# A hybrid decoder step on one core: the last 288 tokens of the end turned with tokens on partitions, h fetched back tile by tile, and the key row rooms given back later

## The chip, the cores and the metric

The program runs on one core of a Trainium2 chip. The metric is the time of one execution of the whole program in microseconds (us). TensorE (PE), VectorE (DVE), ScalarE (ACT) and GpSimd (POOL) each run their own stream of instructions in order; SyncE (SP) issues nearly all the transfers.

## The reference

One layer of a decoder for 512 prompt tokens, 32 sample tokens (8 sequences of 4) and 16 meta tokens, 560 in all, with a model width of 1024:

```python
h = x + 0.5 * rms_norm(swiglu(rms_norm(x, ffn1_pre_g), ...ffn1...), ffn1_post_g)
u = rms_norm(h, mix_pre_g); proj = u @ w_in
# a gated linear attention branch and a stick-breaking attention branch over proj
m = sigmoid(gate_a) * (o_a @ w_o_gla) + sigmoid(gate_b) * (o_b @ w_o_sb)
h = h + rms_norm(m @ w_out, mix_post_g)
y = h + 0.5 * rms_norm(swiglu(rms_norm(h, ffn2_pre_g), ...ffn2...), ffn2_post_g)
```

with `rms_norm(x, g) = x * rsqrt(mean(x*x) + eps) * g` over the width. Outputs are y of the prompt and of the samples (the meta tokens have none), the new keys and values, and the states of the linear attention. Only the last line, the fetch of h ahead of the two `h + ...` sums of the feed-forward blocks, and the writing of the new keys are touched here.

## The kernel before

Activations lie transposed: the width is cut into eight tiles of 128 partitions (`k` = 0 to 7, `hT[k]`), and the tokens are the columns (`NT` = 560 in the first block; `NW` = 544 from the mixer on, as the meta tokens end there). Every product in full precision is three TensorE matmuls of float32r operands split in a high and a low part (lines 681 to 697 and 1145 to 1147), so TensorE runs through the whole program.

The work on PE, DVE, ACT and POOL is in an order written out by hand (`tc.manual_schedule`): a matmul loop calls `step()` after each k-tile, and `later(n, f)` lets `f` emit its instructions n steps on; `flush()` steps until the list is empty. SP is not in that list: the order of the transfers in its queue is set by the framework's scheduler, and the queue itself is in order, so a transfer whose room or buffer isn't free yet holds those behind it.

On-chip room comes from an `Arena` of 150 units of 280 columns in chunks of six. `take(width)` hands out the free units that were given back longest ago, preferring single holes for single units; `give` returns them. A new user of a room waits for the last readers of it.

**Fetching h back.** While the feed-forward block runs, h lies in DRAM (`h_dram`). Both down projections (`Down.pair` for output tiles 2 and 3, and 4 and 5 in the second block; then `k_steps` loops of 22 steps for each remaining output tile and half of the tokens) call `h_again` two steps after the last pair: it takes three rooms and issues the eight loads of `hT[k]` (128x560, 280 KB each) at once, line 1191. The weights of the down projection come through three `raw` buffers (line 185); ACT copies a buffer to a high part (line 660) and DVE makes the low part (line 152).

**The end.** The tokens are in two halves of 272 columns. For each output tile n and half h, `Norm.tile` squares the product (ACT, line 739), scales it by the gain (ACT, line 740) into y, and DVE adds up the squares. When the last tile of a half is there, `start` sums the squares over the partitions with two matmuls against ones (lines 756 and 757; the sum comes out repeated on all partitions), ACT takes Ln and Exp(-0.5 ...) (lines 759 and 760), and for each of three sets of k-tiles (3, 3 and 2) `add` multiplies y by 1/rms and adds it to h on DVE (line 152). `out(j, g)` then turns 128 tokens j of set g on PE (line 2531), copies the turned rows out of PSUM (line 2532, ACT but for one) and writes them (line 2534). In the first half all this lies under the matmuls of tiles 7 and 6 of the second half. For the second half it comes after the last matmul: `start(1)`, and three times an `add` and the turns of token blocks 2, 3 and the 32 samples.

**Key rows.** In the attention part each pair of heads turns the keys of the 48 sample and meta tokens to rows `tk` (`tails`, lines 1885 to 1890), writes them with two DMAs and gives the room back right behind the issue.

Of the kernel before, what the change touches and what calls it, by code (L numbers as in the profile page):

```python
# [12 lines left out]
AF = mybir.ActivationFunctionType  # L13
ALU = mybir.AluOpType

P = 128
D = 1024
KD = D // P
NP = 512
NS = 32  # L20
NM = 16
NT = NP + NS + NM
HW = NT // 2
# [21 lines left out]
MIXER += [("S", "a", 4), ("R", "p", 2), ("R", "p", 3), ("S", "b", 4), ("S", "a", 6), ("R", "p", 4), ("R", "p", 5), ("S", "b", 6)]  # L45
MIXER += [("R", "p", 6), ("R", "p", 7)]
AHEAD = 150
SPREAD = 15
UNITS = 150


class Arena:
# [6 lines left out]
    def __init__(self, pool, n):  # L59
        self.pool, self.clock, self.made = pool, 0, 0  # L60
        self.freed = [[0] * self.CHUNK for _ in range(n // self.CHUNK)]
        self.tile = [None] * len(self.freed)
        self.held = {}
        self.keep = 0

    def take(self, width, dt=F32, tight=False):
        k = -(-width // self.UNIT)
        best = None
        empties = sum(None not in f for f in self.freed)
        for c, free in enumerate(self.freed):  # L70
            empty = None not in free
            if not empty and self.tile[c].dtype != dt:
                continue
            for s in range(self.CHUNK - k + 1):
                f = free[s : s + k]
                if None in f:
                    continue
                since = max(f) if not empty else max(free) + SPREAD
                waste = k % 2 == 0 and s % 2
                alone = k == 1 and free[s ^ 1] is not None  # L80
                key = (empty and empties <= self.keep, waste, tight and sum(x is not None for x in free), alone, since)
                if best is None or key < best[0]:
                    best = (key, c, s)
        assert best is not None, f"no room for {width}: {[sum(x is not None for x in f) for f in self.freed]}"
        _, c, s = best
        if None not in self.freed[c] and (self.tile[c] is None or self.tile[c].dtype != dt):
            self.made += 1
            self.tile[c] = self.pool.tile([P, self.CHUNK * self.UNIT], dt, tag=f"room{c}", name=f"room{c}_{self.made}")
        self.freed[c][s : s + k] = [None] * k
        a = self.tile[c][:, s * self.UNIT : s * self.UNIT + width]  # L90
        self.held[id(a)] = (a, c, s, k)
        return a
# [9 lines left out]
    def give(self, *aps):  # L102
        for a in aps:
            _, c, s, k = self.held.pop(id(a))
            self.clock += 1
            self.freed[c][s : s + k] = [self.clock] * k
# [14 lines left out]
def hybrid_step(  # L121
# [8 lines left out]
    nc = tc.nc  # L130
# [5 lines left out]
    V, S, G, T = nc.vector, nc.scalar, nc.gpsimd, nc.tensor  # L136
    arena = Arena(cp, UNITS)
    take, give = arena.take, arena.give
# [21 lines left out]
    hT, hT_room = whole(KD)  # L160
# [168 lines left out]
    class Head:  # L329
# [246 lines left out]
        def out(self, e):  # L576
            hd, p = self.hd, self.po
            if e < 2:
                oa[hd, e] = take(NP + NS)
                S.activation(oa[hd, e][:, :NP], p, AF.Copy, scale=g_gla[:, e : e + 1])  # L580
            else:
                for e in range(2):
                    S.activation(oa[hd, e][:, NP:], p[:, NS * e : NS * e + NS], AF.Copy, scale=g_gla[:, e : e + 1])
                give(*self.on)
# [132 lines left out]
    def later(n, f):  # L717
        todo.append([n, f])

    def flush():  # L720
        while todo:
            step()

    class Norm:
# [37 lines left out]
        def add(self, h, g):  # L762
# [5 lines left out]
            if g == 2:  # L768
                give(self.rs[h])

    class Gain:


# [410 lines left out]
        for i in range(len(waiting) + 3):  # L1184
            later(2 * i + 1, lambda: waiting and hidden(*waiting.pop(0), 1, nw, wid, hid, pairs))

    def h_again():
        nonlocal hT_room
        hT[:], hT_room = whole(KD)
        for k in range(KD):  # L1190
            nc.sync.dma_start(hT[k], h_dram[k])

    class Down:

# [160 lines left out]
    with tc.manual_schedule(engines={E.PE, E.DVE, E.Activation, E.Pool}):  # L1355
# [167 lines left out]
        for n, hs, j in by_chunks(order1):  # L1523
            if hs is None:
                down1.pair(n, ("ps", "acc"), True)
                later(2, h_again)
                continue
            if j == 0:
                accs[n, hs] = {h: ps("acc") for h in hs}
            acc, (k0, k1) = accs[n, hs], CUTS[j]  # L1530
            if j == 0 and n in EARLY and hs != (1,):
                st.fetch_early(*vrows[EARLY[n]])
            if (n, hs) == (7, (1,)):
                parts = last[j]
            else:
                parts = last[j] = st.parts.pop(0)

            ahead_ = {(7, (0,)): (1, 0, 0), (7, (1,)): (0, 1, 1), }.get((n, hs), (1, 1, 1))
            for _ in range(ahead_[j]):
                st.split()  # L1540
                st.fetch()
            k_steps(acc, parts, k0, k1, KF, hid, hs)
            if j < 2:
                continue
            for h in hs:
                later(1, lambda n=n, h=h, acc=acc: n1.tile(n, h, acc[h]))
            if (n, hs) == (7, (0,)):
                later(2, exp_ln_table)
            for h in range(2):
                if (n, hs) == ((7, (0,)), (4, (1,)))[h]:  # L1550
                    for k in range(KF):
                        give(*hid.t[k, h])
                    todo.extend([d, f] for d, f in g1.pieces(n1, h, *(F0, F1)[h]))
# [189 lines left out]
    class Pair:  # L1743
# [133 lines left out]
        def tails(self):  # L1877
            pr, kf, vf = self.pr, self.kf, self.vf
            p = ps()
            T.transpose(p[:NTL, :P], kf[:, :NTL], ident)  # L1880
            T.transpose(p[:NTL, P : 2 * P], vf[:, NP:], ident)
            T.transpose(p[:, 2 * P : 3 * P], vfm[pr % 2], ident)
            fc = slice(P * (pr % 4), P * (pr % 4) + P)
            self.vm = vm = take(P)
            tk = take(P)
            V.tensor_copy(tk[:NTL], p[:NTL, :P])
            c = slice(self.c0, self.c0 + P)
            nc.sync.dma_start(k_sample.rearrange("o b t h d -> (o b t) (h d)")[:, c], tk[:NS])
            nc.sync.dma_start(kp_out[:NM, c], tk[NS:NTL])
            give(tk)  # L1890
            V.tensor_copy(tail_v[pr // 4][:NTL, fc], p[:NTL, P : 2 * P])
            V.tensor_copy(vm, p[:, 2 * P : 3 * P])
            give(kf, vf)
# [402 lines left out]
    with tc.manual_schedule(engines={E.PE, E.DVE, E.Activation, E.Pool}):  # L2296
# [220 lines left out]
        early_tiles(u2, rs2, W2, NW, hid, pairs, {(0, 0): 9, (1, 0): 9}, lambda: next(feed2))  # L2517
        list(feed2)

        nd, last, accs = Norm(half2, (NW // 2, NW // 2)), {}, {}  # L2520
        down2 = Down(hid, NW, nd)
        down2.pieces(*DSUMS2)
        ys = y_sample.rearrange("b t d -> (b t) d")

        def out(j, g):

            n, ks = P if j < 4 else NS, Norm.SETS[g]
            w = P * len(ks)
            p, t = ps(), take(3 * P)
            for i, k in enumerate(ks):  # L2530
                T.transpose(p[:n, P * i : P * i + P], hT[k][:, P * j : P * j + n], ident)
            (V.tensor_copy if g == 2 and j == 3 else S.copy)(t[:n, :w], p[:n, :w])
            c = slice(P * ks[0], P * ks[0] + w)
            nc.sync.dma_start(y_prompt[0, P * j : P * j + n, c] if j < 4 else ys[:, c], t[:n, :w])

        for n, hs, j in by_chunks(order2):
            if hs is None:
                down2.pair(n, ("ps", "acc") if n == 2 else ("acc", "ps"), n == 4)
                if n == 4:
                    later(2, h_again)  # L2540
                continue
            if j == 0:
                accs[n, hs] = {h: ps("ps" if (n, hs) == (6, (0,)) else "acc") for h in hs}
            acc, (k0, k1) = accs[n, hs], CUTS[j]
            if (n, hs) == (7, (1,)):
                parts = last[j]
            else:
                parts = last[j] = st.parts.pop(0)
            for _ in range({(7, (0,)): (1, 0, 0), (7, (1,)): (0, 1, 1)}.get((n, hs), (1, 1, 1))[j]):
                ahead()  # L2550
            k_steps(acc, parts, k0, k1, KF, hid, hs, wid=nd.wid)
            if j < 2:
                continue
            for h in hs:
                later(1, lambda n=n, h=h, acc=acc: nd.tile(n, h, acc[h]))
            if (n, hs) == (7, (0,)):
                later(2, exp_ln_table)
                later(F1[0], lambda: nd.start(0))
                for g in range(3):
                    later(F1[1] + 9 * g, lambda g=g: nd.add(0, g))  # L2560
                    for j in range(2):
                        later(F1[1] + 9 * g + 7 + 4 * j, lambda j=j, g=g: out(j, g))
        for p in pairs.values():
            give(*p)
        later(2, lambda: nd.start(1))
        for g in range(3):
            later(3 + g, lambda g=g: (nd.add(1, g), [out(j, g) for j in (2, 3, 4)]))
        flush()


# [30 lines left out]
```

## Time and profile before

| | |
|---|---|
| Time, median of 3 runs | 1509.87 us (1509.79 to 1510.43) |
| The profiled execution | 1510.1 us |
| Its span, first to last instruction | 1508.4 us |
| Granted TensorE clock, mean | 0.999 |
| Busy: PE, DVE, ACT, POOL | 1494.6, 1090.8, 773.3, 149.0 us |
| Last matmul of the down projection ends | 1495.1 us after the start of the span |

The profiled execution takes 1.7 us more than its span, and 0.2 us more than the median of the runs. Times inside a trace are counted from the start of its span. A row of the chain or the timeline has the start, the length, the engine, the line and what was written from what; in brackets stands the idle time before it and what ended that. A row of a group has its count, its busy time in us and the mean of one in ns. In the windows the last three numbers are the clock granted to TensorE, the share of the DMA engines and GB/s.

### The profile page before, as it was taken

What the parts mean: (1) busy time and instruction counts of PE and PEld (TensorE: products, weight loads), DVE (VectorE), ACT (ScalarE), POOL (GpSimd) and SP (SyncE); (2) the same over time, 40 slices, a digit from 0 to 9 for tenths busy, and PEclk for the clock granted to TensorE, in tenths of its full rate; (3) what the DMA queues carried; (4) which work ended last, traced back from release to release, by engine and by line L of the source; (5) the groups of instructions that cost most, each with busy time, mean ns of one, the idle gap of its engine ahead of it and who ended that gap; (6) DMA issues with size and microseconds to landing.
All of it is one profiled execution on the core that took longest, in us unless ns stands there. A gap on an engine that the chain in (4) does not pass through costs nothing.

```text
span 1508.4 us, 29660 instructions
## 1 busy us (share of the span) xinstructions
PE 1494.6 (99%) x11923; PEld 1440.9 (96%) x11923; DVE 1090.8 (72%) x1934; ACT 773.3 (51%) x1425; POOL 149.0 (10%) x216
## 2 busy tenths in 40 slices
PE   9999999999999999999999999999999999999997
PEld 8999999999999889899888899999999999999997
DVE  5888888853787867877776434977567898888544
ACT  6455454533665557565555343634565555455333
POOL 2000000000000011123324541000000000000000
PEclk9999999999999999999999999999999999999999
DMA  8133333336565473334555568335531333332352
GB/s 250 53 88 99 98 98 97 88 103 193 155 158 149 121 110 85 91 85 115 128 107 141 177 202 196 92 99 144 156 107 67 99 98 99 99 110 87 94 163 85
DMA packets 276794, 180.40 MB, mean 120 GB/s; under 512 B 10202, under 2 KB 261648, under 8 KB 276656
## 3 DMA queue, kind: packets, MB, share of 16 engines
q1 hardware_dynamic: 271200, 161.64, 40.6%
q0 software_dynamic: 5440, 16.85, 3.3%
q8 instruction: 94, 1.54, 0.4%
q14 instruction: 44, 0.36, 0.1%
q10 hardware_dynamic: 16, 0.00, 0.0%
HBM read 155.72 MB, written 22.74 MB: 118 GB/s over the span
## 4 chain that ended last, share of the span: by engine, by line
PE 95%; DVE 2%; DMA 1%; ACT 1%; issue 0%; ACTq 0%; DVEq 0%; SPq 0%
PE acc L681 8%; PE acc L1147 8%; PE acc L1145 8%; PE acc L682 8%; PE acc L684 8%; PE acc L1146 8%; PE acc L694 7%; PE acc L697 7%; PE acc L695 7%; PE acc L1088 2%; PE acc L1085 2%; PE acc L1086 2%; PE acc L925 1%; PE acc L927 1%; PE acc L926 1%; PE ps L1920 1%
## 5 line engine op out<-in xcount | busy, mean ns | idle before, releaser
L152 DVE TENSOR_TENSOR lo<-raw,hi 128x1024 fp32r<-128x1024 f32 (+1 forms) x213 | 254.9, 1197 | 127.5 <-ACT hi L660 104.1
L152 DVE TENSOR_TENSOR room<-room,room 128x544 fp32r<-128x544 f32 (+17 forms) x419 | 266.2, 658 | 89.1 <-ACT room L760 27.9
L681 PE MATMUL acc<-room,hi 128*128 128x280 f32 (+1 forms) x928 | 271.2, 309 | 0.2 <-DVE room L155 0.2
L1147 PE MATMUL acc<-room,lo 128*128 128x280 f32 (+1 forms) x896 | 259.8, 290 | 0.0
L1146 PE MATMUL acc<-room,hi 128*128 128x280 f32 (+1 forms) x896 | 259.2, 289 | 0.0
L1145 PE MATMUL acc<-room,hi 128*128 128x280 f32 (+1 forms) x896 | 259.1, 289 | 0.0
L682 PE MATMUL acc<-room,hi 128*128 128x280 f32 (+1 forms) x928 | 250.4, 289 | 0.0
L684 PE MATMUL acc<-room,lo 128*128 128x280 f32 (+1 forms) x928 | 192.7, 289 | 0.0
L681 PEld LDWEIGHTS acc<-room,hi 128*128 128x128 f32 x928 | 174.8, 188 | 13.1 <-issue 11.0
L682 PEld LDWEIGHTS acc<-room,hi 128*128 128x128 f32 x928 | 175.1, 189 | 2.8 <-issue 1.9
L1147 PEld LDWEIGHTS acc<-room,lo 128*128 128x128 f32 x896 | 168.6, 188 | 0.0
L1145 PEld LDWEIGHTS acc<-room,hi 128*128 128x128 f32 x896 | 168.5, 188 | 0.0
L1146 PEld LDWEIGHTS acc<-room,hi 128*128 128x128 f32 x896 | 168.5, 188 | 0.0
L856 ACT CAST hi<-raw 128x1024 fp32r<-128x1024 f32 x92 | 96.4, 1052 | 133.1 <-PE acc L1146 48.7
L660 ACT CAST hi<-raw 128x1024 fp32r<-128x1024 f32 (+1 forms) x121 | 122.6, 1014 | 71.2 <-DMA raw<-in_ffn_w_down_dram 21.0
L684 PEld LDWEIGHTS acc<-room,lo 128*128 128x128 f32 x928 | 145.0, 188 | 0.0
L694 PE MATMUL acc<-room,hi 128*128 128x280 f32 (+2 forms) x498 | 143.0, 294 | 0.3 <-ACT hi L660 0.3
L695 PE MATMUL acc<-room,hi 128*128 128x280 f32 (+2 forms) x498 | 140.9, 290 | 0.0
L697 PE MATMUL acc<-room,lo 128*128 128x280 f32 (+2 forms) x498 | 127.8, 291 | 1.3 <-DVE lo L152 1.3
L856 ACT CAST hi<-room 128x1024 fp32r<-128x1024 f32 x84 | 70.2, 836 | 81.0 <-PE acc L1146 59.1
L694 PE MATMUL acc<-room,room 128*128 128x280 f32 (+3 forms) x366 | 107.8, 295 | 0.0
L152 DVE TENSOR_TENSOR lo<-room,hi 128x1024 fp32r<-128x1024 f32 x84 | 80.2, 955 | 37.0 <-ACT hi L856 36.8
(381 smaller groups left out, 3290.7 us busy)
## 6 DMA issues: line engine op xcount, KB each, us to landing
raw<-in_w_in_dram SPq DMA_DIRECT2D x49, 512.0 KB
raw<-in_ffn_w_down_dram SPq DMA_DIRECT2D x40, 448.0 KB
raw<-in_ffn_w_gate_dram SPq DMA_DIRECT2D x64, 256.0 KB
raw<-in_ffn_w_up_dram SPq DMA_DIRECT2D x64, 256.0 KB
out_dram<-room SPq DMA_DIRECT2D x32, 256.0 KB
raw<-in_ffn_w_down_dram SPq DMA_DIRECT2D x14, 512.0 KB
raw<-in_w_in_dram SPq DMA_DIRECT2D x28, 256.0 KB
h_dram<-room SPq DMA_DIRECT2D x24, 280.0 KB
```

Of the source, the lines that this page charges most:

```text
L152: (eng or V).tensor_tensor(out=out, in0=a, in1=b, op=op)
L660: S.copy(h_, src)
L681: T.matmul(acc[h][:, : wid[h]], hi[k], a[h][0], start=(k == 0), stop=False)
L682: T.matmul(acc[h][:, : wid[h]], hi[k], a[h][1], start=False, stop=False)
L684: T.matmul(acc[h][:, : wid[h]], lo[k], a[h][0], start=False, stop=(k == KD - 1))
L694: T.matmul(acc[h][:nw, : wid[h]], wh, a[h][0], start=(k == 0), stop=False)
L695: T.matmul(acc[h][:nw, : wid[h]], wh, a[h][1], start=False, stop=False)
L697: T.matmul(acc[h][:nw, : wid[h]], wl, a[h][0], start=False, stop=(k == kt - 1))
L856: S.copy(hi[:, :kt], src)
L1145: T.matmul(x[:, :QW], hi, act[k][0], start=(first and k == 0), stop=False, skip_group_check=True)
L1146: T.matmul(x[:, :QW], hi, act[k][1], start=False, stop=False, skip_group_check=True)
L1147: T.matmul(x[:, :QW], lo, act[k][0], start=False, stop=(k == 3), skip_group_check=True)
```

## The change

- `Last` takes the place of `Norm` in the second feed-forward block. Its y and sums of squares cover all 544 columns in shared rooms. The first part (`start`, `add` with columns 0 to 255, `out` for token blocks 0 and 1) is done where it was, for 256 columns instead of 272.
- The last 288 columns are done in `end`, behind the last matmul: the token blocks A (256 to 383) and B (384 to 511) and the samples C (512 to 543). h is turned by itself into SBUF (`x_turned`), y is turned by itself and stays in PSUM (`turned(y_at, ...)`). The squares of a token are summed by a matmul with the squares as the stationary operand and one column of ones, which gives one value per token on that token's partition, and one DVE instruction per 512 columns makes `y * rs + x` from PSUM and SBUF, written out as 128 rows of 512. Only the samples are multiplied and added as before (32 columns), turned, copied and written in two pieces.
- The last square goes with a DVE instead of an ACT scaling of y.
- `h_again(every)` spreads the eight loads: one each 8 steps in the first block, one each 5 steps in the second.
- `tk` is given back 12 steps later.

```diff
@@ -45,6 +45,7 @@
 MIXER += [("S", "a", 4), ("R", "p", 2), ("R", "p", 3), ("S", "b", 4), ("S", "a", 6), ("R", "p", 4), ("R", "p", 5), ("S", "b", 6)]
 MIXER += [("R", "p", 6), ("R", "p", 7)]
 AHEAD = 150
+LEAVE = 12
 SPREAD = 15
 UNITS = 150
 
@@ -768,6 +769,108 @@
             if g == 2:
                 give(self.rs[h])
 
+    class Last:
+
+        A = 2 * P
+
+        def __init__(self, post, w):
+            self.wid, self.w, self.post, self.n, self.y, self.q = (w, w), w, post, [0, 0], {}, {}
+
+        def view(self, g):
+            return self.y[g].rearrange("p (k t) -> p k t", t=NT)
+
+        def tile(self, n, h, acc):
+            w, g = self.w, n // 3
+            c = slice(h * w, h * w + w)
+            if g not in self.y:
+                self.y[g] = take(len(Norm.SETS[g]) * NT)
+            self.n[h] += 1
+            what = {1: "sum", KD: "last"}.get(self.n[h])
+            if what:
+                if what not in self.q:
+                    self.q[what] = take(NT)
+                q = self.q[what][:, c]
+            else:
+                q_ = take(HW)
+                q = q_[:, :w]
+            S.activation(q, acc[:, :w], AF.Square)
+            y = self.view(g)[:, n % 3, c]
+            if h and self.n[h] == KD:
+                V.tensor_scalar(out=y, in0=acc[:, :w], scalar1=self.post[:, n : n + 1], scalar2=None, op0=ALU.mult)
+            else:
+                S.activation(y, acc[:, :w], AF.Copy, scale=self.post[:, n : n + 1])
+            if not what:
+                tt(self.q["sum"][:, c], self.q["sum"][:, c], q, ALU.add)
+                give(q_)
+
+        def start(self):
+            w = self.A
+            rs = self.rs = take(w)
+            p = ps()
+            T.matmul(p[:, :w], ones, self.q["sum"][:, :w], start=True, stop=False)
+            T.matmul(p[:, :w], ones, self.q["last"][:, :w], start=False, stop=True)
+            S.activation(rs, p[:, :w], AF.Ln, bias=epst, scale=1.0 / D)
+            S.activation(rs, rs, AF.Exp, scale=-0.5)
+
+        def add(self, g, c, rs):
+            n = len(Norm.SETS[g])
+            y, x = self.view(g)[:, :, c], hT_room[g].rearrange("p (k t) -> p k t", t=NT)[:, :n, c]
+            tt(y, y, rs.unsqueeze(1).to_broadcast([P, n, c.stop - c.start]), ALU.mult)
+            tt(x, x, y, ALU.add)
+
+        def end(self, prompt, samples):
+            def turned(src, c, n, w):
+                p = ps("acc")
+                for i in range(4):
+                    T.transpose(p[:n, P * i : P * i + P], src(4 * w + i)[:, c : c + n], ident)
+                return p
+
+            def x_at(k):
+                return hT[k]
+
+            def y_at(k):
+                return self.view(k // 3)[:, k % 3]
+
+            def x_turned(c):
+                t = take(D)
+                for w in range(2):
+                    p = ps()
+                    for i in range(4):
+                        T.transpose(p[:, P * i : P * i + P], hT[4 * w + i][:, c : c + P], ident)
+                    S.copy(t[:, 512 * w : 512 * w + 512], p)
+                return t
+
+            def out(c, w, y, x, r):
+                o = take(512)
+                stt(o, y, r, x[:, 512 * w : 512 * w + 512], ALU.mult, ALU.add)
+                nc.sync.dma_start(prompt[c : c + P, 512 * w : 512 * w + 512], o)
+
+            A, B, C = self.A, self.A + P, NP
+            q, rs = self.q["sum"], take(P)
+            xa = x_turned(A)
+            tt(q[:, A:NW], q[:, A:NW], self.q["last"][:, A:NW], ALU.add)
+            ya = [turned(y_at, A, P, 0)]
+            p = ps()
+            for i, c in enumerate((A, B)):
+                T.matmul(p[:, i : i + 1], q[:, c : c + P], ones[:, :1], start=True, stop=True)
+            T.matmul(p[:, 2 : 2 + NS], ones, q[:, C:NW], start=True, stop=True)
+            S.activation(rs[:, : 2 + NS], p[:, : 2 + NS], AF.Ln, bias=epst, scale=1.0 / D)
+            S.activation(rs[:, : 2 + NS], rs[:, : 2 + NS], AF.Exp, scale=-0.5)
+            ya.append(turned(y_at, A, P, 1))
+            out(A, 0, ya[0], xa, rs[:, 0:1])
+            xb = x_turned(B)
+            out(A, 1, ya[1], xa, rs[:, 0:1])
+            for g in range(3):
+                self.add(g, slice(C, NW), rs[:, 2 : 2 + NS])
+            yb = [turned(y_at, B, P, w) for w in range(2)]
+            pc = [turned(x_at, C, NS, w) for w in range(2)]
+            out(B, 0, yb[0], xb, rs[:, 1:2])
+            for w in range(2):
+                t = take(512)
+                S.copy(t[:NS], pc[w][:NS])
+                nc.sync.dma_start(samples[:, 512 * w : 512 * w + 512], t[:NS])
+            out(B, 1, yb[1], xb, rs[:, 1:2])
+
     class Gain:
 
 
@@ -1184,11 +1287,11 @@
         for i in range(len(waiting) + 3):
             later(2 * i + 1, lambda: waiting and hidden(*waiting.pop(0), 1, nw, wid, hid, pairs))
 
-    def h_again():
+    def h_again(every):
         nonlocal hT_room
         hT[:], hT_room = whole(KD)
         for k in range(KD):
-            nc.sync.dma_start(hT[k], h_dram[k])
+            later(1 + every * k, lambda k=k: nc.sync.dma_start(hT[k], h_dram[k]))
 
     class Down:
 
@@ -1523,7 +1626,7 @@
         for n, hs, j in by_chunks(order1):
             if hs is None:
                 down1.pair(n, ("ps", "acc"), True)
-                later(2, h_again)
+                later(2, lambda: h_again(8))
                 continue
             if j == 0:
                 accs[n, hs] = {h: ps("acc") for h in hs}
@@ -1887,7 +1990,7 @@
             c = slice(self.c0, self.c0 + P)
             nc.sync.dma_start(k_sample.rearrange("o b t h d -> (o b t) (h d)")[:, c], tk[:NS])
             nc.sync.dma_start(kp_out[:NM, c], tk[NS:NTL])
-            give(tk)
+            later(LEAVE, lambda: give(tk))
             V.tensor_copy(tail_v[pr // 4][:NTL, fc], p[:NTL, P : 2 * P])
             V.tensor_copy(vm, p[:, 2 * P : 3 * P])
             give(kf, vf)
@@ -2517,27 +2620,27 @@
         early_tiles(u2, rs2, W2, NW, hid, pairs, {(0, 0): 9, (1, 0): 9}, lambda: next(feed2))
         list(feed2)
 
-        nd, last, accs = Norm(half2, (NW // 2, NW // 2)), {}, {}
+        nd, last, accs = Last(half2, NW // 2), {}, {}
         down2 = Down(hid, NW, nd)
         down2.pieces(*DSUMS2)
         ys = y_sample.rearrange("b t d -> (b t) d")
 
         def out(j, g):
 
-            n, ks = P if j < 4 else NS, Norm.SETS[g]
+            ks = Norm.SETS[g]
             w = P * len(ks)
             p, t = ps(), take(3 * P)
             for i, k in enumerate(ks):
-                T.transpose(p[:n, P * i : P * i + P], hT[k][:, P * j : P * j + n], ident)
-            (V.tensor_copy if g == 2 and j == 3 else S.copy)(t[:n, :w], p[:n, :w])
+                T.transpose(p[:, P * i : P * i + P], hT[k][:, P * j : P * j + P], ident)
+            S.copy(t[:, :w], p[:, :w])
             c = slice(P * ks[0], P * ks[0] + w)
-            nc.sync.dma_start(y_prompt[0, P * j : P * j + n, c] if j < 4 else ys[:, c], t[:n, :w])
+            nc.sync.dma_start(y_prompt[0, P * j : P * j + P, c], t[:, :w])
 
         for n, hs, j in by_chunks(order2):
             if hs is None:
                 down2.pair(n, ("ps", "acc") if n == 2 else ("acc", "ps"), n == 4)
                 if n == 4:
-                    later(2, h_again)
+                    later(2, lambda: h_again(5))
                 continue
             if j == 0:
                 accs[n, hs] = {h: ps("ps" if (n, hs) == (6, (0,)) else "acc") for h in hs}
@@ -2555,17 +2658,15 @@
                 later(1, lambda n=n, h=h, acc=acc: nd.tile(n, h, acc[h]))
             if (n, hs) == (7, (0,)):
                 later(2, exp_ln_table)
-                later(F1[0], lambda: nd.start(0))
+                later(F1[0], nd.start)
                 for g in range(3):
-                    later(F1[1] + 9 * g, lambda g=g: nd.add(0, g))
+                    later(F1[1] + 9 * g, lambda g=g: nd.add(g, slice(0, nd.A), nd.rs))
                     for j in range(2):
                         later(F1[1] + 9 * g + 7 + 4 * j, lambda j=j, g=g: out(j, g))
         for p in pairs.values():
             give(*p)
-        later(2, lambda: nd.start(1))
-        for g in range(3):
-            later(3 + g, lambda g=g: (nd.add(1, g), [out(j, g) for j in (2, 3, 4)]))
         flush()
+        nd.end(y_prompt[0], ys)
 
 
 # ---- launch: one core; inputs and outputs as the reference has them ----
```

## The prediction

> **What bounds the kernel now.** I read the page first, then the windows of 20 us for the places where TensorE isn't full, then the timeline around each, and the chain of the last 15 us.
>
> ```profile
> span 1508.4 us, 29660 instructions
> PE 1494.6 (99%) x11923; PEld 1440.9 (96%) x11923; DVE 1090.8 (72%) x1934; ACT 773.3 (51%) x1425; POOL 149.0 (10%) x216
> PE 95%; DVE 2%; DMA 1%; ACT 1%; issue 0%; ACTq 0%; DVEq 0%; SPq 0%
> ```
>
> TensorE bounds the program: 1494.6 of 1508.4 us, and the change takes away no matmul of the body. What it can win is where TensorE stands still, 13.8 us in all. Most of that is the end, and one more place lies in a stage that the change touches:
>
> ```profile
> 320.00:340.00 20.00, 20.00 (x157) 20.00 (x156) 9.99 (x17) 8.41 (x15) 0.00 (x0) 1.00 0.35 102
> 340.00:360.00 20.00, 18.41 (x139) 17.73 (x138) 8.77 (x9) 8.55 (x12) 0.00 (x0) 1.00 0.92 268
> ...
> 342.76 0.40 PE L694 MATMUL acc<-room,hi 128*128 128x280 f32 x1 [0.26 <-ACT hi L660]
> 344.02 0.40 PE L697 MATMUL acc<-room,lo 128*128 128x280 f32 x1 [0.74 <-DVE lo L152]
> 353.36 0.39 PE L697 MATMUL acc<-room,lo 128*128 128x280 f32 x1 [0.59 <-DVE lo L152]
> ```
>
> At 320 to 340 us a matmul takes 20/157 = 0.127 us; the next window holds 18 fewer, so 18 x 0.127 = 2.3 us are lost there, in three waits for weight parts that came late. What made them late are transfers:
>
> ```profile
> 338.00:352.00 14.00, 13.00 (x99) 12.54 (x99) 3.98 (x5) 4.63 (x6) 0.00 (x0) 1.00 1.13 331
> ...
> 339.77 3.54 SPq L1191 DMA_DIRECT2D room<-h_dram  x5
> 343.99 18.22 SPq L185 DMA_DIRECT2D raw<-in_ffn_w_down_dram  x8
> ```
>
> For 14 us the DMA engines are full at 331 GB/s, with five of the eight h loads side by side and the weights (line 185) beside and behind them.
>
> The end, by the chain and the timeline:
>
> ```profile
> 1494.98 0.13 PE acc L697
> 1495.11 0.46 PE ps L756 x2
> 1495.59 0.74 PE ps L757 x2
> 1496.36 0.50 ACT room L759
> 1496.88 0.44 ACT room L760
> 1497.34 1.02 DVE room L152
> 1498.38 1.94 DVE room L152 x2
> 1500.34 1.02 DVE room L152
> 1501.50 3.34 PE ps L2531 x15
> 1504.86 0.36 ACT room L2532
> ...
> 1495.14 0.40 ACT L739 ACTIVATE room<-acc 128x272 f32<-128x272 f32 x1 [1.08 <-PE acc L697]
> 1499.54 1.17 PE L2531 MATMUL ps<-ident,room 128*128 128x128 f32 x9 [3.22 <-DVE room L152]
> 1500.60 5.70 SPq L2534 DMA_DIRECT2D out_dram<-room  x9
> ```
>
> From the last matmul at 1495.11 the steps stand in a row: sum, Ln, Exp (until 1497.31), DVE passes over 816 columns before anything can be turned, the turns, the copies. The last copy ends at 1505.22, and the span 3.2 us later, with SP issuing until 1506.3.
>
> **The end, step by step.** The new end turns y and h before 1/rms is known, so only one DVE pass per 512 columns stands behind it. The prices:
>
> ```profile
> L1862 ACT COPY room<-ps 128x512 f32<-128x512 f32 x8 | 4.7, 588 | 3.0 <-PE ps L1860 2.5 <-ACT hi L660 0.4
> L556 ACT ACTIVATE st<-st,epst 128x4 f32<-128x4 f32 x4 | 1.2, 300 | 0.1
> L2532 ACT COPY room<-ps 32x384 f32<-32x384 f32 x2 | 0.9, 467 | 0.2 <-PE ps L2531 0.2
> L557 ACT ACTIVATE st<-st 128x4 f32<-128x4 f32 x4 | 0.8, 208 | 0.1
> L2532 ACT COPY room<-ps 32x256 f32<-32x256 f32 x1 | 0.4, 362 | 0.4 <-PE ps L2531 0.4
> ...
> L152 DVE TENSOR_TENSOR room<-room,acc 128x272 f32<-128x272 f32 x98 | 41.1, 433 | 20.5 <-PE acc L927 10.2 <-PE acc L1147 8.7 <-PE acc L1311 1.3
> L155 DVE SCALAR_TENSOR_TENSOR room<-room,room,ps 128x256 f32<-128x256 f32 x32 | 13.9, 477 | 12.3 <-PE ps L522 12.3
> L155 DVE SCALAR_TENSOR_TENSOR room<-room,gains,room 128x544 f32<-128x544 f32 x8 | 6.2, 780 | 0.0
> L152 DVE TENSOR_TENSOR room<-room 128x32 f32<-128x32 f32 x4 | 0.7, 184 | 0.0
> L152 DVE TENSOR_TENSOR room<-room,gains 128x128 f32<-128x128 f32 x1 | 0.3, 294 | 3.3 <-DMA room<-in_w_in_dram 3.3
> ```
>
> *Up to 1/rms.* The square ends at 1495.54 (0.40). DVE scales y beside it (0.43, to 1495.6) and adds the last square to the sum (288 columns, 0.45, to 1496.05). PE meanwhile turns 8 tiles of h and 4 of y; nine turns took 1.17 us, 0.11 a turn and a last latency of 0.27, so 12 x 0.11 = 1.3 after 1495.1, to 1496.45. The turns hide the add, and ACT copies the turned h (2 x 0.59, to 1496.9) beside them. The three sum products are tiny, two passes each (as x2 in the chain for one product); I have no row of one column against a full stationary operand, so I bound it: 6 x 0.11 as turns below, and above the 1.2 us of the two wide products in the chain. I take 0.9, nearer to the turns, as the weights are what is loaded: 1497.35. Ln 0.30 and Exp 0.21 at four columns, with gaps: **1/rms at 1497.9**, 0.6 later than before.
>
> *DVE from there.* Four passes of 512 columns: 256 cost 0.48 and 544 cost 0.78, so 0.75 each, 3.0. Six sample passes of 96, 96 and 64 columns, between 0.18 and 0.29, 1.45 together. With ten gaps of 0.02 that is 4.65: **the last pass ends at 1502.55**, against 1505.22. Queued in front of block B's passes are the sample passes; nobody else needs DVE.
>
> *What must keep up.* PE has 8 turns of h and 12 of y left after the sums, 20 x 0.11 = 2.2, to 1499.7, ahead of block B's passes at 1500.9. The turns of the samples wait for their adds (1500.9) and end by 1501.7; ACT copies two pieces of 32x512 (0.47 + 0.105 = 0.57 each), to 1502.3, beside the last passes. PSUM's four rooms per kind suffice but for the samples, which reuse block A's, free by 1499.4. So DVE is the bound, with 0.25 to spare to ACT.
>
> *SP and the landing.* Six writes instead of nine; the last is 256 KB and not 32. Before, 3.2 us lie between the last copy and the end, 1.1 of them SP's: its own issue and about one ahead (nine in 5.70 us, 0.63 each). After, a sample piece is ahead at most, up to 0.3 less, and 224 KB more at the 331 GB/s above cost up to 0.7 more. No row shows exactly this; from 0.3 less to 0.7 more, I take 0.4 more, nearer to the bytes, as they must all move: the end at 1502.55 + 3.6 = 1506.1, with 1505.2 and 1507.2 as the sum's ends. **Gain of the end: 2.3 us (1.2 to 3.2).** The first half's adds run over 768 instead of 816 columns under matmuls: nothing.
>
> **The fetch of h.** In block one a tile each 8 steps is 24 matmuls or 3.05 us: 287 KB per 3.05 us is 94 GB/s, beside weights of 1.44 MB per 22 steps (8.4 us), 172 GB/s. Together 266, under the 331 that the queues moved. Then no weight is late and the 2.3 us come back. In block two it is 287 KB per 1.9 us, 151 + 172 = 323, just under; nothing stalled there before:
>
> ```profile
> 1445.70 0.81 SPq L1191 DMA_DIRECT2D room<-h_dram  x2
> ```
>
> But this row is a warning: the call stands after the pair that ends at 1459 us, and two loads went out 14 us before it. The scheduler moves loads ahead as soon as their room is free, whatever step emits them. So the gain lies between 0 and 2.3 us; I take 1.7, since in block one five of the eight came late and in one heap, where order decides. Below nothing: SP's queue is in order, and an h load that waits for its room could hold weights; that costs at most a stall such as those above, 0.3 to 0.7.
>
> **Key rooms.** No wait for `tk`'s room appears on an engine, so the edit wins nothing by itself. It deals out all later rooms anew. Nearest is a wait of another room for an output transfer:
>
> ```profile
> POOL room L1703 <- DMA out_dram<-room: 5.8, 1, 5.8
> ```
>
> I take 0; both ends stay: a few tenths less, 5.8 more.
>
> **Sum.** Profiled 1510.1 - 2.3 - 1.7 = 1506.1; the median stood 0.2 lower, so 1505.9.
>
> **A rule against it.** The clock of the turns, three half-microsecond windows of the end:
>
> ```profile
> 1501.00:1501.50 0.50, 0.00 (x1) 0.04 (x1) 0.50 (x2) 0.30 (x1) 0.00 (x0) 0.68 0.09 34
> 1503.50:1504.00 0.50, 0.50 (x4) 0.50 (x3) 0.00 (x0) 0.34 (x2) 0.00 (x0) 0.50 0.44 169
> 1504.50:1505.00 0.50, 0.33 (x3) 0.00 (x0) 0.42 (x1) 0.14 (x1) 0.00 (x0) 0.91 0.92 332
> ```
>
> After PE had stood idle, the 15 turns ran at half clock, 3.34/15 = 0.22 each, and after 3.3 us of nothing but turns it was back. So turns keep the clock up, and the new end, which turns almost without a break, should stay at full clock until 1499.7. The Trainium skill, "TensorE: Matmul & The Clock Gate", section "Part 4: PE-mode transpose", says that the full clock "doesn't engage for transpose-mode", as such work isn't counted as busy. The trace disagrees; by that rule the late turns would run at half clock, which is the third case below.
>
> **The rivals.**
> *The loads keep their order* (0.25). For it speaks the load 14 us ahead of its call; against it the heap of five. Only the end gains: 1507.6, of measure no change: this kernel's measurement can tell 0.2%, 3.0 us.
> *The end runs cold or in a longer row* (0.12). If the sample turns run at 0.22 (+0.9), or block B's turns of y wait for the samples' adds in the same room, the second sample piece and the write queued behind it go out some 0.9 later: 1506.8.
> *A room comes round too early* (0.09). Rooms dealt anew let a load in SP's queue wait for a room that an output transfer still reads, 5.8 us by the row. The weights behind it are late, PE waits as long, and the gain of the h loads is gone too: 1509.9 - 2.3 + 5.8 = 1513.4. It decides from a wait of 2.3 us on, where the end's gain is used up. Against it: of PE's 13.8 us of idle time 7.6 lie behind 1495.1 (13.3 less 0.46, 0.74, 1.17 and 3.34 of work) and 1.6 in the window at 340, so that 4.6 are left for the whole rest, start included.
>
> **How the numbers follow.** My forecast, both gains, 0.54: 1505.9, with its own range 1504.2 to 1508.0 from the terms. The second case adds 1506.7 to 1508.7, the third lies inside; the range 1503.8 to 1509.2 leaves out most of the fourth and the far tails. Faster by over 0.2% (below 1506.85) are 0.44 of the first case, 0.05 of the second and 0.07 of the third: 0.56. Slower (above 1512.9) are 0.06, most of the fourth; the rest, 0.38, lies within.
>
> **What would show it.** Right: no PE wait at 340 to 360 us and 157 matmuls in that window; h loads one by one between weight loads; after the last matmul Exp ends 2.8 us on, the last DVE pass 7.4 us on, the end 11 us on instead of 13.3; clock 1.00 until block B is turned. Wrong: five h loads in one heap again, an Exp later than 3.5 us, turns of 0.22 us before 1499.7, or a new PE wait anywhere between 600 and 1495 us.

## The result, and the profile after

| | median | lowest to highest |
|---|---|---|
| before, 21 runs | 1510.19 us | 1509.79 to 1511.51 |
| changed, 21 runs | 1507.44 us | 1506.73 to 1509.79 |
| ratio | 0.9981 | 0.9975 to 0.9987 (95%) |

The change makes the kernel 0.19% faster, 2.8 us. That lies in the predicted range, 1.5 us above the predicted time and 0.2 us from the time of the first rival, in which only the end gains (1507.6). So the time alone doesn't tell the forecast from that rival. The execution whose trace is read here took 1508.72 us, 1.3 more than the median of the changed kernel; where that may come from is told below.

The page of the changed kernel, span and busy times:

```profile
span 1507.0 us, 29698 instructions
PE 1494.2 (99%) x11941; PEld 1442.1 (96%) x11941; DVE 1090.0 (72%) x1939; ACT 771.5 (51%) x1422; POOL 149.3 (10%) x216
```

TensorE is still the bound. Next the chain of the changed kernel from the last matmul on:

```profile
1495.67 0.14 PE acc L698
...
1495.84 0.41 ACT room L796
...
1496.27 0.50 DVE room L799
1496.77 0.37 DVE room L153
...
1497.28 0.58 PE ps L855 x4
1497.85 0.26 PE ps L856 x2
...
1498.14 0.30 ACT room L857
...
1498.46 0.24 ACT room L858
...
1498.73 1.41 DVE room L156 x2
...
1501.37 0.74 DVE room L156
```

The row of steps is the forecast one: square (line 796), the y scaling and the add of the last square on DVE, the sum products, Ln, Exp, then nothing but DVE. The last matmul ends at 1495.67 + 0.14 = 1495.81 and the span at 1507.0: 11.2 us, where it was 13.3. What remains after the last matmul is 2.1 us shorter.

The timeline of the changed kernel's end, DVE's last two rows and SP's:

```profile
1500.05 1.39 DVE L153 TENSOR_TENSOR room<-room,room 128x96 f32<-128x96 f32 x6
1501.37 1.40 DVE L156 SCALAR_TENSOR_TENSOR room<-acc,room,room 128x512 f32<-128x512 f32 x2
...
1502.04 0.33 SPq L871 DMA_DIRECT2D out_dram<-room  x1
1502.47 0.36 SPq L846 DMA_DIRECT2D out_dram<-room  x1
1503.24 0.33 SPq L871 DMA_DIRECT2D out_dram<-room  x1
1503.68 0.36 SPq L846 DMA_DIRECT2D out_dram<-room  x1
```

DVE works without a gap from 1498.73 to 1502.77. The last write is issued 0.9 us after that, behind a sample piece (line 871).

The fetch of h in block one. The window of the changed kernel:

```profile
340.00:360.00 20.00, 18.37 (x129) 17.90 (x128) 7.93 (x9) 8.28 (x11) 0.00 (x0) 0.91 0.91 264
```

PE's waits in the second window, from its timeline:

```profile
343.11 0.40 PE L695 MATMUL acc<-room,hi 128*128 128x280 f32 x1 [0.90 <-ACT hi L661]
...
344.37 0.40 PE L698 MATMUL acc<-room,lo 128*128 128x280 f32 x1 [0.73 <-DVE lo L153]
```

And SP's rows there:

```profile
330.91 0.34 SPq L1294 DMA_DIRECT2D room<-h_dram  x1
...
331.77 0.50 SPq L1294 DMA_DIRECT2D room<-h_dram  x1
333.59 0.37 SPq L186 DMA_DIRECT2D raw<-in_ffn_w_down_dram  x1
334.00 1.75 SPq L1294 DMA_DIRECT2D room<-h_dram  x1
336.62 3.41 SPq L186 DMA_DIRECT2D raw<-in_ffn_w_down_dram  x2
340.08 1.42 SPq L1294 DMA_DIRECT2D room<-h_dram  x1
344.34 2.37 SPq L186 DMA_DIRECT2D raw<-in_ffn_w_down_dram  x2
346.76 2.98 SPq L1294 DMA_DIRECT2D room<-h_dram  x2
349.91 0.38 SPq L186 DMA_DIRECT2D raw<-in_ffn_w_down_dram  x1
350.34 1.03 SPq L1294 DMA_DIRECT2D room<-h_dram  x2
...
```

The program emits the loads 24 matmuls, or 3.05 us, apart. The queue shows something else: three went out from 330.91 to 334.00, ahead of and among the weight loads, a fourth at 340.08, and two pairs stand later. The heap of five is gone, and with it the wait at 353 us; the pair of waits at 343 and 344 us has stayed, 1.63 us together. So this trace shows no gain here at all: the pair has grown from 1.00 us to 1.63, PE stands still for 1.6 us in the window as before, and it runs 10 matmuls fewer in it than before (129 against 139). Those are a matter of the clock, again by the windows, here cut where the clock changes:

```profile
342.26:345.68 3.42, 1.84 (x12) 1.61 (x13) 1.69 (x2) 1.82 (x3) 0.00 (x0) 1.00 0.82 238
345.68:349.09 3.41, 3.41 (x16) 3.41 (x16) 2.08 (x3) 1.97 (x4) 0.00 (x0) 0.50 0.93 266
```

Behind the two waits the granted clock is 0.50 for 3.4 us. PE is busy, but slow; the first and the last of 13 such matmuls in its timeline:

```profile
345.83 0.43 PE L695 MATMUL acc<-room,hi 128*128 128x280 f32 x1
...
348.63 0.43 PE L695 MATMUL acc<-room,hi 128*128 128x280 f32 x1
```

They start (348.63 - 345.83)/12 = 0.233 us apart instead of 0.127, so 13 of them lose 1.4 us. In no other trace of this study does the clock drop in this stage, though several have a pair of waits there. It would account for the 1.3 us by which this execution stands above the median, but as only one execution has a trace, that is argued and not shown.

### The profile page after: what moved, and what is told of

Same layout as the page of the kernel before. It is cut to its first block, busy times and chain, and to the rows that moved or that the text cites. A ratio compares the mean times of both kernels' runs of the same rounds, so it can differ in the third digit from the quotient of the medians.

```text
span 1507.0 us, 29698 instructions
## 1 busy us (share of the span) xinstructions
PE 1494.2 (99%) x11941; PEld 1442.1 (96%) x11941; DVE 1090.0 (72%) x1939; ACT 771.5 (51%) x1422; POOL 149.3 (10%) x216
## 4 chain that ended last, share of the span: by engine, by line
PE 94%; DVE 2%; DMA 2%; ACT 1%; issue 0%; DVEq 0%; SPq 0%; ACTq 0%
PE acc L682 8%; PE acc L1248 8%; PE acc L1249 8%; PE acc L685 8%; PE acc L683 8%; PE acc L1250 8%; PE acc L695 7%; PE acc L698 7%; PE acc L696 7%; PE acc L1191 2%; PE acc L1188 2%; PE acc L1189 2%; PE acc L1028 1%; PE acc L1029 1%; PE acc L1030 1%; PE ps L2023 1%
## 5 line engine op out<-in xcount | busy, mean ns | idle before, releaser
L153 DVE TENSOR_TENSOR room<-room,room 128x544 f32<-128x544 f32 (+17 forms) x413 | 259.0, 649 | 81.4 <-ACT room L740 15.0
L661 ACT CAST hi<-raw 128x1024 fp32r<-128x1024 f32 (+1 forms) x121 | 122.7, 1015 | 72.0 <-DMA raw<-in_ffn_w_down_dram 18.6
```

Source lines behind the costliest of these rows:

```text
L153: (eng or V).tensor_tensor(out=out, in0=a, in1=b, op=op)
L661: S.copy(h_, src)
```

## The experiments

The first four ran on one chip and the others on a second; on both the kernel before takes 1505.5 us, not the 1510.2 of the comparison above (28 runs beside the first four, 22 beside the others, medians 1505.50 and 1505.55). The changed kernel itself would take 0.9981 x 1505.5 = 1502.6 there.

**The three parts, each by itself.** The theory: the end brings 2 us and the spread loads less than forecast. The rivals: the loads bring most, or the key rooms do.

The end alone, which is the changed kernel with two edits undone:

```diff
-            later(1 + every * k, lambda k=k: nc.sync.dma_start(hT[k], h_dram[k]))
+            nc.sync.dma_start(hT[k], h_dram[k])
...
-            later(LEAVE, lambda: give(tk))
+            give(tk)
```

> The changed kernel with all eight loads of h issued at once in both blocks and the key row room given back at once: the new end alone. Theory 1 (the end carries the gain, the spread loads bring nothing, since three of the eight loads still stand ahead of the weight load that is late): 2.1 us below before, the 13.3 us behind the last matmul against 11.2 in the changed kernel's trace; some 1508.1. Theory 2 (the spread loads bring a part, about 1 us): the end alone brings 1.7 at most, above 1508.4.

Measured: 1503.26 us (11 runs), ratio 0.9985 [0.9976, 0.9994], 2.2 us less than before.

The spread loads alone, put into the kernel before:

```diff
-            nc.sync.dma_start(hT[k], h_dram[k])
+            later(1 + every * k, lambda k=k: nc.sync.dma_start(hT[k], h_dram[k]))
...
-                later(2, h_again)
+                later(2, lambda: h_again(8))
...
-                    later(2, h_again)
+                    later(2, lambda: h_again(5))
```

> The kernel before with only the loads of h spread (8 and 5 steps). Theory 1: same as before within 0.4 us; the wait at 342 to 344 us stays, the one at 353 us goes, and TensorE's clock may drop after the first. Theory 2: 1 us or more below before.

Measured: 1504.72 us (11 runs), ratio 0.9995 [0.9986, 1.0004], 0.8 us less; the interval takes in no difference. Its waits of PE at 340 to 360 us, from the timeline, are the first pair alone:

```profile
342.13 0.40 PE L694 MATMUL acc<-room,hi 128*128 128x280 f32 x1 [0.46 <-ACT hi L660]
343.39 0.40 PE L697 MATMUL acc<-room,lo 128*128 128x280 f32 x1 [0.73 <-DVE lo L152]
```

The end alone, whose loads all go out at one step, has such a pair and behind it one more in its timeline:

```profile
...
353.42 0.40 PE L698 MATMUL acc<-room,lo 128*128 128x280 f32 x1 [0.69 <-DVE lo L153]
```

So what the spreading takes away in the traces is the wait at 353 us, of 0.7 us. The measured 0.8 agrees with it, though by itself it could be nothing.

The key rooms alone, in the kernel before:

```diff
-            give(tk)
+            later(12, lambda: give(tk))
```

> The kernel before with only the key row room given back 12 steps later. Both theories: same as before within 0.4 us. The rival that rooms dealt anew shift waits in the body: 0.5 us or more either way.

Measured: 1505.04 us (11 runs), ratio 0.9997 [0.9988, 1.0006]: no difference that these runs can tell. The three parts make 2.2 + 0.8 + 0.5 = 3.5 us where the whole has 2.9 by its ratio, which is within their intervals.

**Why the first pair of waits stays.** The theory: on SP's queue the scheduler lets a load go out as soon as its room is free, whatever step emits it, and the loads that stand ahead of weight loads make these late. Two rivals: the bytes are too many for the window in whatever order, or the weights are late for a reason of their own. The test gives the loads of block one to the queue of ScalarE, whose order is the one written by hand:

```diff
-    def h_again(every):
+    def h_again(every, queue=None):
...
-            later(1 + every * k, lambda k=k: nc.sync.dma_start(hT[k], h_dram[k]))
+            later(1 + every * k, lambda k=k: (queue or nc.sync).dma_start(hT[k], h_dram[k]))
...
-                later(2, lambda: h_again(8))
+                later(2, lambda: h_again(8, nc.scalar))
```

> The changed kernel with the h loads of block one issued by ScalarE, whose order is written out by hand, so that they really go out one each 8 steps behind its other work. Theory 1: the weight load behind them is on time, no TensorE wait at 340 to 360 us, 2 us below the changed kernel (1505.4). Rival (the sum of the bytes is too much for the DMA engines, whatever the order): waits of 1.5 us or more stay and the time is the changed kernel's within 0.4 us; issuing costs ScalarE 0.4 us each but hides.

Measured: 1500.40 us (6 runs), ratio 0.9965 [0.9952, 0.9977]. The window and, from ACT's timeline, the first and the last of the eight issues:

```profile
340.00:360.00 20.00, 20.00 (x158) 20.00 (x157) 8.76 (x9) 8.44 (x12) 0.00 (x0) 1.00 1.00 287
```

```profile
335.94 0.36 ACTq L1294 DMA_DIRECT2D room<-h_dram  x1
...
354.71 0.33 ACTq L1294 DMA_DIRECT2D room<-h_dram  x1
```

TensorE has no wait left: 158 matmuls in 20 us at clock 1.00. More bytes move in that window than in the changed kernel's (287 against 264 GB/s), so it wasn't the bytes. An issue costs ACT 0.33 to 0.36 us, which nobody waits for here.

It could still be that a second queue is what helps, and not the order. So the loads stayed on SP, each held behind the weight load that was emitted last before it:

```diff
+    fetched = []
...
-        nc.sync.dma_start(raw, w[r0 : r0 + kt * P, c0 : c0 + nw].rearrange("(k p) n -> p k n", p=P))
+        fetched.append(nc.sync.dma_start(raw, w[r0 : r0 + kt * P, c0 : c0 + nw].rearrange("(k p) n -> p k n", p=P)))
...
-            later(1 + every * k, lambda k=k: nc.sync.dma_start(hT[k], h_dram[k]))
+            def load(k=k):
+                if every == 8:
+                    with tc.issue_after(fetched[-1].ins):
+                        nc.sync.dma_start(hT[k], h_dram[k])
+                else:
+                    nc.sync.dma_start(hT[k], h_dram[k])
+            later(1 + every * k, load)
```

> The changed kernel with each h load of block one queued on SP behind the weight load emitted last before it, so that one h load stands between two weight loads and none ahead of the first three. Theory 1 (the order in SP's queue is all that was missing): as with ScalarE's queue, no TensorE wait at 340 to 360 us and 2.2 us below the changed kernel. Rival (ScalarE's own queue was what helped, as a second ring runs beside SP's): the wait at 342 us stays and the time is the changed kernel's within 0.5 us.

Measured: 1501.12 us (7 runs), ratio 0.9971 [0.9960, 0.9982]. The window, and SP's first rows there:

```profile
340.00:360.00 20.00, 20.00 (x158) 20.00 (x157) 9.86 (x10) 9.30 (x13) 0.00 (x0) 1.00 0.98 297
```

```profile
333.90 4.76 SPq L188 DMA_DIRECT2D raw<-in_ffn_w_down_dram  x3
338.72 0.56 SPq L1300 DMA_DIRECT2D room<-h_dram  x1
341.85 0.37 SPq L188 DMA_DIRECT2D raw<-in_ffn_w_down_dram  x1
342.26 0.57 SPq L1300 DMA_DIRECT2D room<-h_dram  x1
...
```

One h load stands between two weight loads, from the first on, on the same queue as before, and again no wait is left. That settles it for this stage: the h loads that stood ahead of the weights in the queue made these late, and neither their bytes nor the lack of a second queue. Against the changed kernel's 1502.6 or so the two versions have 2.2 and 1.6 us less; their intervals overlap, so which of the two is better isn't told by these runs.

**Is the last microsecond SP's?** Before the last write SP issues a sample piece. The theory: taking the samples' writes from SP lets the last write go out half a us earlier, and the end follows. The rival: the bytes of the writes and their landing set the end.

```diff
-                nc.sync.dma_start(samples[:, 512 * w : 512 * w + 512], t[:NS])
+                nc.scalar.dma_start(samples[:, 512 * w : 512 * w + 512], t[:NS])
```

> The changed kernel with the two sample pieces issued by ScalarE behind its copies instead of by SP. Theory 1 (at the very end SP's issuing sets the end: the last DVE pass ended 0.9 us before the last issue began, as three issues of 0.43 to 0.77 us stood in front): 0.7 us below the changed kernel, the last prompt piece issued within 0.3 us of its pass. Rival (the writes' bytes and their landing set the end): the same within 0.3 us.

Measured: 1502.44 us (11 runs), ratio 0.9980 [0.9971, 0.9989], as the changed kernel's. In its trace SP issues the last two prompt pieces one behind the other, and then the DMA engines are busy:

```profile
1495.62 0.99 SPq L846 DMA_DIRECT2D out_dram<-room  x2
```

```profile
1496.50:1498.50 2.00, 0.00 (x0) 0.00 (x0) 0.00 (x0) 0.02 (x1) 0.00 (x0) 0.73 0.92 285
```

The last DVE pass ends at 1496.26 there and SP's last issue at 1496.61, 0.35 behind it instead of 1.27 (1504.04 against 1502.77). But the last bytes move some 2.6 us behind that pass in both traces, at 1498.9 here and at 1505.4 in the changed kernel. So it was not SP; with the DMA engines 92% busy for 2 us, the bytes of the four pieces take this time, as the rival has it. The same edit on the version with ACT's loads:

> The changed kernel with the h loads of block one and the two sample pieces issued by ScalarE. If the two gains stand apart, as they lie 1100 us from each other: 2.2 and 0.7, 2.9 us below the changed kernel, 5.8 below before. Rival (samples bring nothing): 2.2 below the changed kernel.

Measured: 1500.90 us (7 runs), ratio 0.9970 [0.9958, 0.9981]: not below the 0.9965 without it. Beside the 1502.44 of the same chip, where the two kernels differ by ACT's loads alone, it is 1.5 us less, which repeats what these are worth. Then the six sample passes went to GpSimd besides, to let DVE end earlier:

```diff
-                self.add(g, slice(C, NW), rs[:, 2 : 2 + NS])
+                self.add(g, slice(C, NW), rs[:, 2 : 2 + NS], G)
...
-            tt(y, y, rs.unsqueeze(1).to_broadcast([P, n, c.stop - c.start]), ALU.mult)
-            tt(x, x, y, ALU.add)
+            tt(y, y, rs.unsqueeze(1).to_broadcast([P, n, c.stop - c.start]), ALU.mult, eng)
+            tt(x, x, y, ALU.add, eng)
```

> The last one with the six sample passes (multiply and add of 32 columns per k-tile) on GpSimd instead of VectorE. Theory 1 (VectorE's passes set the end): block B's two passes start 1.4 us earlier and the end comes up to 1.2 us earlier, if the samples keep up. Rival (GpSimd is slower and the sample pieces become last): the same within 0.4 us, or up to 1 us later.

Measured: 1501.43 us (8 runs), ratio 0.9974 [0.9964, 0.9985], no gain either. Its timeline shows that the work itself does end earlier:

```profile
1490.18 2.73 DVE L156 SCALAR_TENSOR_TENSOR room<-acc,room,room 128x512 f32<-128x512 f32 x4 [1.60 <-ACT room L858]
1490.29 2.26 POOL L153 TENSOR_TENSOR room<-room,room 128x96 f32<-128x96 f32 x6 [577.45 <-ACT room L858]
...
1493.91 0.34 ACTq L871 DMA_DIRECT2D out_dram<-room  x1
```

The four passes stand in one row and end 2.7 us after 1/rms, not 4.0. The bytes end earlier too, in this window:

```profile
1495.00:1495.50 0.50, 0.00 (x0) 0.00 (x0) 0.00 (x0) 0.00 (x0) 0.00 (x0) 1.00 0.36 127
```

That is 8.1 us behind the last matmul of this trace (1495.4 against 1487.26). In the changed kernel it is 9.6 (1505.4 against 1495.81):

```profile
1505.00:1505.50 0.50, 0.00 (x0) 0.00 (x0) 0.00 (x0) 0.00 (x0) 0.00 (x0) 1.00 0.51 193
```

Yet the span ends at 1499.5, some 4 us behind the bytes and not 1.6. What lies between are rows of line 2698, the statement in which the whole program stands and which closes it: a drain of every engine and semaphores between them. They don't count as busy, but the view of that line has them, with the count, the shortest, median and longest in ns, and the start of the first and of the last. First the version with GpSimd, then the changed kernel:

```profile
L2698 POOLq EVENT_SEMAPHORE  x4: 17/17/17, 1498.7 to 1499.4; - x4
L2698 POOLq DRAIN  x3: 46/93/6490, 1492.2 to 1499.2; - x3
L2698 SPq DRAIN  x3: 7/7/129, 1496.3 to 1499.0; - x3
```

```profile
L2698 POOLq EVENT_SEMAPHORE  x4: 17/17/17, 1506.3 to 1506.9; - x4
L2698 POOLq DRAIN  x3: 46/93/18557, 917.5 to 1506.7; - x3
L2698 SPq DRAIN  x3: 7/7/7, 1506.2 to 1506.5; - x3
```

In the changed kernel GpSimd's long drain begins at 917.5 us, about where its work ends, takes 18.6 us and is long over; its first semaphore comes 0.1 us behind SP's first drain. In the version with GpSimd's adds that drain begins at 1492.2 and lasts 6.49 us, and only then, at 1498.7, comes GpSimd's semaphore, 2.4 us behind SP's drain. So this run doesn't speak against the theory: in its trace a shorter row on DVE does end the bytes some 1.5 us earlier, and GpSimd's drain takes the gain back. Whether the time falls by as much when the samples' adds leave DVE and GpSimd stays idle, no run shows; nor what a drain of GpSimd does for so long.

The lowest ratio is that of the changed kernel with ScalarE's queue for the loads of block one, 0.9965 [0.9952, 0.9977] of before; the runs don't tell it from the 0.9970 and 0.9971 above.

## Why the prediction was right or wrong

*The end, forecast 2.3.* Right: 2.1 by the traces, 2.2 by the end alone. Its steps, counted from the last matmul: Exp ends at 2.9 (forecast 2.8), the last DVE pass at 7.0 (7.4), the span at 11.2 (11.0). The sizes behind that: the sum products took 0.58 + 0.26 = 0.84 (0.9, taken near the turns, not the 1.2 of the wide ones), a 512-column pass 0.70 (0.75), the six sample passes 1.39 with hardly a gap (1.45 and gaps). Two steps were off and cancel in part. DVE's scaling of y doesn't run beside the Square but behind it (1496.27, where the Square ends at 1496.24); the turns hid all but 0.17 us of that, as PE had until 1497.1 to turn. And the landing: from the last pass to the end it is 4.2 us, not 3.6. SP does issue the second sample piece ahead of the last write, which begins 0.9 after the pass, but without that piece on SP it is 4.3 (1496.26 to 1500.6). The term was taken nearer to the bytes, and that was the right side: they end the same 2.6 us behind the pass.

*The rule against it.* At every window from 1498 to 1501.5 the changed kernel's clock is 1.00 while TensorE does little but turn, and eight turns take 1.04 us; the first of those windows:

```profile
1498.00:1499.00 1.00, 1.00 (x11) 1.00 (x11) 0.27 (x1) 0.52 (x2) 0.00 (x0) 1.00 0.00 0
...
```

From 1499.38 to 1502.79 it does nothing but turn, 2.10 us of 3.41, and the clock is still 1.00 until 1506.2. The third case, turns at half clock, did not come. By the rule of the Trainium skill, "TensorE: Matmul & The Clock Gate", section "Part 4: PE-mode transpose", it should have; the trace again disagrees.

*The loads, forecast 1.7 of a possible 2.3.* This is the term that was mis-sized: 0.8 measured, with an interval that takes in nothing and 2.1. The sign named for it, no wait at 340 to 360 us and 157 matmuls there, did not come: two waits and 129 matmuls. The step that failed is the choice between the bounds, "in block one five of the eight came late and in one heap, where order decides". The heap did go, but it caused only the wait at 353 us. The two waits at 342 to 344 us come from the loads ahead of the heap, and those went out early again, as the load sent 14 us ahead of its call at 1445 us had warned. The mechanism of the first rival, that the loads keep their order, held for three loads of eight. The 2.3 itself holds: the three waits are only 1.59 us, but the window lacked 18 matmuls, and with the loads on ScalarE's queue it has 158 instead of 139. The bandwidth sum was right, and this is why the forecast's full 2.3 can be had once the queue has the order that the program emits: 1.5 to 2.2 on top of the change.

*Key rooms, forecast 0.* Right, as far as 0.5 with an interval of 1.4 us both ways can tell. No new wait of an engine for an output transfer came up (GpSimd's one of 5.8 us is 4.9 in the changed kernel), so the rival that ends slower found nothing to stand on.

*The sum.* From the 1510.19 us that before took in the comparison, 2.3 and 1.7 off give 1506.2; measured are 1507.44, 1.2 more: 0.9 of the loads' term, 0.2 of the end's, and the rest below what the runs tell. That the time fell into the range all the same is owed to its width: it held the first rival's time too.

## What to carry to other kernels

Spreading transfers over the steps of a loop only paces them if the queue keeps the order in which they are emitted: read the issues' times and their places among the other loads in the trace, not the program. Where a scheduler may send a load early, hold it behind the load that must go first, or put it in the queue of an engine whose order is written by hand. At the end of a program, look at the rows of its last line too: an engine that works there still has to drain, which took GpSimd 6.49 us here. And where a change has several parts, run each alone: here the end brought three quarters of the gain, one brought about a third of what it could, and one nothing that can be measured.

## What the runs showed of the hardware that was not expected

- Two waits of 0.90 and 0.73 us, some 1.2 us from one to the next, were followed once by 3.4 us at clock 0.50 (345.68 to 349.09 us, changed kernel); in the kernel with the key rooms alone waits of 1.19 and 0.73 us at 353 to 355 us were followed by none. The ten traces have a pattern for this: their clock changes only at multiples of 3.41 us from its first change. Up to the drop, one such step (342.26 to 345.68) holds both waits, and TensorE is busy for 1.84 us of it; in the other kernel a boundary at 352.88 cuts through the first wait, and TensorE is busy for 2.59 us of the step before it and 2.32 of the one behind. Wherever TensorE had stood still for 1.58 us or more of a step at full clock, the next step had 0.50; up to 1.48 us, it had 1.00. No run was made to test this.
- GpSimd's drain in the kernel's last line took 6.49 us in the version with GpSimd's adds, where the end waited for it, and 18.6 us, hidden under other work, in the changed kernel.
- Two products of one column against a full 128x128 stationary operand, of two passes each, took 0.58 us. From start to start a pass took 0.11 us (1497.28 to 1497.72 for four), as a turn did.
- Six small passes (96 and 64 columns) took 2.26 us on GpSimd and 1.39 on DVE.
